# First outputs' chunks taken alternately, a seventh pair by seven products, and the last norm's shift and stores in quarters

## The chip, the cores and the metric

The kernel runs on one core of one Trainium2 chip. The metric is the device time of one execution in microseconds (us). Three runs of the kernel before took 716.66, 716.94 and 717.12 us. PE is TensorE (PEld its weight loads), DVE is VectorE, ACT is ScalarE, POOL is GpSimd, SP is the engine that issues most of the DMAs; each engine works through its own instructions in the order in which they were written.

## The reference

Two decoder layers over 256 tokens of width 1024, in float32:

```python
for l in range(DEPTH):                       # DEPTH = 2, x is (1, 256, 1024)
    mix = hybrid_mixer(x, w_in[l], w_branch_sb[l], w_branch_moba[l], w_out[l])
    x = layer_norm(ALPHA * x + mix, ln_mix_g[l], ln_mix_b[l])
    ffn = (silu(x @ w_gate[l]) * (x @ w_up[l])) @ w_down[l]      # inner width 2816
    x = layer_norm(ALPHA * x + ffn, ln_ffn_g[l], ln_ffn_b[l])
```

`hybrid_mixer` projects x to q, k, v of eight stick-breaking heads, q, k, v of eight softmax heads and two gates; each attention goes through its own output projection, the two are merged by the sigmoid gates and go through `w_out`. Nearly all of the time is in products of x, or of what was made of it, with weights.

## The kernel before

**Products.** Every float32 operand is split into a high part (cast to float32r, on ACT) and a low part (the rest, subtracted on DVE). A product is made of three matmuls: high with high, high with low, low with high (`mm3`). Tiles of 128 tokens are called t = 0 and t = 1.

**The weight stream.** The weights come in granules of 128 x 1024 numbers (512 KB), 122 of them a layer; `g` numbers them in the order of use, and `place` gives where a granule lies in memory. `WeightStream.load` issues the load of a granule into one of six raw tiles (`NRAW`) on SP's queue; `WeightStream.line` casts it on ACT into `whi` and subtracts on DVE into `wlo`, rings of ten granules each. A raw tile is free for the next load when its granule is split, a ring place when PE has used its granule. A few granules (`BY_DMA`) are split by DMA instead (`dma_line`): POOL issues a load into the high part, ACT makes its negative in the low part, and POOL issues a second load that adds the weights to it. `ASIDE` lists chunks of the last stage that are made in the same way, into other places than the ring; it is empty.

**The order of work** is fixed when the program is written: `Weave` keeps an estimate of each engine's time and emits side work (splits, loads, norms, attention) between the products when its due time has come. Nothing is reordered on the chip.

**Start.** x comes transposed in pieces (`xT_raw`; `x10` in `START` is token tile 1, piece 0). Four pieces go by ACT's queue, and then ACT loads its table for a first activation; the other two go by SP's. `START` is the order in which x's pieces and the halves of the first granules (`w10` is granule 1, half 0) are split. The first products are v of the stick-breaking heads (`pv`, granules 0 to 3) and then v of the other heads (`pu`, granules 4 to 7), each for both token tiles. `NWHOLE` = 1: granule 0 is multiplied unsplit, as float32, by `whole`.

**The last stage of a layer** multiplies the 22 chunks of h (128 of the 2816 inner columns each) with `w_down`. `DOWN[l]` is the order: an integer is a chunk taken singly (12 matmuls of 512 columns for each token tile's two halves together), a pair is taken by seven products instead of eight (21 matmuls instead of 24). For a pair the stream has the granules b and a, then two tiles of sums of halves, t and u, made on DVE by four additions of 512 columns (`raw<-raw`); of a only half is split. Sums of the two chunks of h are made on DVE earlier, as soon as both are there (`sums_line`). The last `HOLD[l]` chunks are kept for the end, where each token tile takes them by itself, so that the norm of tile 0 can start while PE works on tile 1. After the last pair, `combine_line` adds the seven products on DVE into x. The h tiles `h_t[i]` hold chunks 4i to 4i + 3, as a high and a low tile. The tiles of the norm's scale and shift, `ln` (`load_gb`), come from the same rotating pool of twelve as the twelve h tiles and are asked for right behind them; their loads are queued on SP when the sixth entry of `DOWN[l]` is reached (`n == 5`).

**The end.** `last_first` is the last norm of tile 0, `last_second` that of tile 1: x plus the products, statistics on DVE, a power on POOL, one scaling pass and one pass that multiplies and shifts (`x<-x,l1b_ve,ln`), each in two halves of 512 columns, and each half is stored by SP.

Of the kernel before, what the change touches and what calls it, by code (L numbers as in the profile page):

```python
# [7 lines left out]
F32 = mybir.dt.float32  # L8
F32R = mybir.dt.float32r
BF16 = mybir.dt.bfloat16  # L10
AF = mybir.ActivationFunctionType
OP = mybir.AluOpType
# [3 lines left out]
P = 128  # L16
# [14 lines left out]
GCOLS = 1024  # L31
NG_LAYER = 122
DOWN = ((0, (4, 5), (6, 7), 1, (8, 9), 2, (10, 11), 3, (12, 13), 14, 15, 16, 17, 18, 19, 20, 21),
        (0, (4, 5), (6, 7), 1, (8, 9), 2, (10, 11), 3, (12, 13), 16, (14, 15), 17, 18, 19, 20, 21))
STEPS = [[e for d in down for e in
          ([("n", d)] if isinstance(d, int) else [("b", d[1]), ("a", d[0]), ("t", d[0]), ("u", d[0])])]
         for down in DOWN]
BASE = [sum(NG_LAYER - NFC + len(x) for x in STEPS[:l]) for l in range(DEPTH + 1)]
EARLY = [*range(4), *range(16, 20), 8, 14, 9, 15, *range(4, 8), 20, 24, 21, 25, *range(10, 14), 22, 23,
         *range(26, 40)]  # L40
NACT = 12
# [67 lines left out]
class WeightStream:  # L109
# [2 lines left out]

    def __init__(self, nc, pool, w, total, weave, rings):
        self.nc, self.pool, self.w, self.total, self.weave = nc, pool, w, total, weave
        self.loaded, self.split = 0, NWHOLE
        self.done = -1
        self.free = {-1: 0.0}
        self.current = 0
        self.rings = rings
        self._lay()  # L120
        self.dma_t = 1.7
        self.raws, self.left = [], {0: 9.0}
        self.raw, self.parts, self.there, self.ready, self.dma = {}, {}, {}, {}, {}
# [50 lines left out]
    def by_dma(self, g):  # L174

        l, r = where(g)
        return r < NG_LAYER - NFC and r in BY_DMA[l] or self.aside(g)

    def aside(self, g):

# [3 lines left out]

    def put_aside(self, l, places):

        for g, parts in zip(filter(self.aside, range(BASE[l], BASE[l + 1])), places):
            self.parts[g] = parts
            self.dma[g] = self.weave.add(self.dma_line(g), self.weave.t)

    def dma_line(self, g):

        nc, weave = self.nc, self.weave
        hi, lo = self.parts[g]
        nc.gpsimd.dma_start(hi, self.w[place(g)], max_dma_last_dim=4096)
        yield weave.t + DMA_HI
        if self.aside(g):
            e = weave.pool(weave.t, nc.gpsimd.tensor_scalar, lo, hi.bitcast(F32), -1.0, None, op0=OP.mult) + 2.7
        else:
            e = weave.act(weave.t, GCOLS, nc.scalar.mul, lo, hi.bitcast(F32), -1.0)  # L200
        yield e
        nc.gpsimd.dma_start(lo, self.w[place(g)], accum_op=OP.add, max_dma_last_dim=4096)
        self.ready[g] = weave.t + DMA_LO

# [56 lines left out]
    def piece(self, g, i, e):  # L261

        if i == 0:
            self.parts[g] = tuple(ring[:, self.place[g]:self.place[g] + GCOLS] for ring in self.rings)
        (hi, lo), t, sl = self.parts[g], self.raw[g], self._pieces(g)[i]
        n = sl.stop - sl.start
        e = self.weave.act(e, n, self.nc.scalar.copy, hi[:, sl], t[:, sl])
        self.ready[g] = self.weave.dve(e, n, self.nc.vector.tensor_sub, lo[:, sl], t[:, sl], hi[:, sl].bitcast(F32))
        if sl.stop == GCOLS:
            self.raw.pop(g)  # L270
            self.left[g] = self.ready[g]
            self.split += 1
            self.load(g + 1 + NRAW)

# [6 lines left out]
    def take(self, g):  # L281
# [3 lines left out]
        while g in self.dma and g not in self.ready:  # L285
# [6 lines left out]
RING = 10 * GCOLS + LINES  # L292
NRAW = 6
NWHOLE = 1
START = (("x00", 4.4), ("x10", 5.4), ("x01", 6.4), ("w10", 6.4), ("w11", 7.4), ("x11", 7.4), ("w20", 8.2), ("x02", 9.0),
         ("w21", 9.7), ("x12", 10.3), ("w30", 11.0), ("w31", 11.7))
BY_DMA = ((18, 24, 28, 33, 38), (18, 24, 28, 33, 38))
ASIDE = ((), ())
X_AFTER = {(2, 0): (0, 2), (2, 1): (1, 2)}
NSPLIT = 10  # L300
HOLD = (8, 5)
FINE = 4
N_WARM = 10
LEAD = 2
# [14 lines left out]
def place(g):  # L319

    l, r = where(g)
    if r >= NG_LAYER - NFC:
        r = NG_LAYER - NFC + STEPS[l][r - (NG_LAYER - NFC)][1]
    return l * NG_LAYER + (EARLY[r] if r < len(EARLY) else r)


# [35 lines left out]
def hybrid_trunk_kernel(ctx: ExitStack, tc: tile.TileContext, w, xT_in, x_in, ln_in,  # L362
# [134 lines left out]

    kcs = [slice(0, 2), slice(2, 4), slice(4, 8)]
    ws.side = weave.add(ws.line(), last=True)
    for t, k in ((0, 0), (1, 0), (0, 1), (1, 1)):  # L500
        load_xT(t, kcs[k], nc.scalar)
    nc.scalar.activation(warm, zero, AF.Sigmoid)

    def between(g, i):
        if (g, i) in X_AFTER:
# [61 lines left out]

    def tok_major(o, g, t, first, last, k0):

        if g < NWHOLE:  # L570
            return whole(o, g, t, first)
        hi, lo = ws.take(g)
        hi = hi.rearrange("p (k c) -> p k c", k=2)
        lo = lo.rearrange("p (k c) -> p k c", k=2)
        for k in range(2):
            ts = slice(t * P, (t + 1) * P)
            mm3(o, xT_hi[:, k0 + k, ts], xT_lo[:, k0 + k, ts], hi[:, k, :], lo[:, k, :],
                first and k == 0, last and k == 1)

    def both_tokens(name, g0, put):  # L580

        acc = [banksB(f"{name}{t}")[:, 0, :] if g0 == 4 else bankM(f"{name}{t}", [P, WIDTH]) for t in range(2)]
        order = ((0, 0), (1, 0), (0, 1), (1, 1), (0, 2), (1, 2), (0, 3)) if g0 <= 4 else \
            ((0, 0), (0, 1), (0, 2), (1, 0), (1, 1), (0, 3), (1, 2))
        for t, k in order + ((1, 3),):
            tok_major(acc[t], g0 + k, t, k == 0, k == 3, 2 * k)
            if t == 1:
                ws.used(g0 + k)
            if k == 3:
                put(t, acc[t])  # L590

    def feat_major(o, g):

# [296 lines left out]
    def last_second(name, banks, gb, down):  # L890

        x = xs[1]
        st = small.tile([P, 3, 6], F32, tag="bn", name=f"{name}_bn1", bufs=1)
        mv = small.tile([P, 2], F32, tag="mv", name=f"{name}_mv1", bufs=1)
        ve = small.tile([P, 1], F32, tag="ve", name=f"{name}_ve1")
        cols = [halves[0], slice(512, 768), slice(768, 1024)]
        (_, first), (_, second) = banks
        rest = bankC(f"{name}_rest", [P, 512])[:, :256]
        down([(0, first)])
        residual(pe_done(), x, cols[0], first, scale=1.0)  # L900
        dve(0.0, 512, nc.vector.bn_stats, st[:, 0, :], x[:, cols[0]])
        down([(512, second)], NFC - HOLD[-1], NFC - FINE, last=False)
        down([(512, second[:, :256])], NFC - FINE)
        residual(pe_done(), x, cols[1], second[:, :256], scale=1.0)
        dve(0.0, 256, nc.vector.bn_stats, st[:, 1, :], x[:, cols[1]])
        residual(pe_done(), x, cols[2], second[:, 256:], scale=1.0)
        down([(768, rest)], NFC - FINE, first=True)
        dve(pe_done(), 256, nc.vector.tensor_add, x[:, cols[2]], x[:, cols[2]], rest)
        e = dve(0.0, 256, nc.vector.bn_stats, st[:, 2, :], x[:, cols[2]])
        e = dve(e, 16, nc.vector.bn_aggr, mv, st[:, :len(cols), :])  # L910
        e2 = dve(e, 16, nc.vector.tensor_scalar, ve, mv[:, 1:2], EPS, None, op0=OP.add)
        e2 = pool(e2, nc.gpsimd.tensor_tensor, ve, ve, mhalf, op=OP.pow)
        g, b = gb
        for c in halves:
            dve(e, 512, nc.vector.scalar_tensor_tensor, x[:, c], x[:, c], mv[:, 0:1], g[:, c], op0=OP.subtract, op1=OP.mult)
        for c in halves:
            dve(e2, 512, nc.vector.scalar_tensor_tensor, x[:, c], x[:, c], ve, b[:, c], op0=OP.mult, op1=OP.add)
            nc.sync.dma_start(out[P:, c], x[:, c])

    def v_parts(name):  # L920
        return [unit(f"{name}{t}", [P, 2 * NPAIR, 2, DH], F32R) for t in range(2)]
# [18 lines left out]
    for l in range(DEPTH):  # L940
# [10 lines left out]
            split_v(v_mb[t], ps)  # L951

        if l == 0:
            both_tokens(f"{L}pv", G, put_v)
            both_tokens(f"{L}pu", G + 4, put_u)
        else:
            for t in range(2):
                weave.finish(norms[:t + 1])
                pe_after(xT_ready[t])
                for j, put in enumerate((put_v, put_u)):  # L960
                    ps = bankM(f"{L}pvu{j}{t}", [P, WIDTH])
                    for i in range(4):
                        g = G + 4 * j + i
                        tok_major(ps, g, t, i == 0, i == 3, 2 * i)
                        if t == 1:
                            ws.used(g)
                    put(t, ps)
# [164 lines left out]

        pairs = [d for d in DOWN[l] if not isinstance(d, int)]
        pair_of = {c: i for i, p in enumerate(pairs) for c in p}
        raw_h, sums, h_there = {}, {}, {}

        def sums_line(i, e):

# [4 lines left out]
                                (3, b0, tmp[:, 1], OP.subtract)):  # L1143
                e = dve(e, P, nc.vector.tensor_tensor, tmp[:, j], x, y, op=op)
            if i < 2:
                both = wide_work(f"{L}hw{i}", F32R).rearrange("p a h c -> p (a h c)")[:, :GCOLS]
            elif i < 4:
                both = work.tile([P, 2, 2, S], F32R, tag=("sbq", "sbk")[i - 2],
                                 name=f"{L}hw{i}").rearrange("p a h c -> p (a h c)")
# [4 lines left out]
            elif i == 5:  # L1154
                places = [[x[:, 0::2, P:] for x in h_t[k]] for k in (1, 2)]
            else:
                places = [[x[:, 6:, :].rearrange("p k (j c) -> p (k j) c", c=P) for x in (xT_hi, xT_lo)]]
            n = 4 // len(places)
            sums[i] = [[hi_lo[m][:, j] for hi_lo in places for j in range(n)] for m in range(2)]
            yield e  # L1160
# [245 lines left out]
```

## Time and profile before

| what | value |
|---|---|
| median of three runs | 716.94 us |
| the profiled execution | 716.68 us, span 714.9 us |
| busy share of the span | PE 99%, PEld 92%, DVE 84%, ACT 61%, POOL 5% |
| granted TensorE clock | 0.997 |
| DMA | 141.58 MB, mean 198 GB/s over the span |

The span runs from the first to the last instruction. Lines of the order of time begin with the start and the length in us, then engine, line of the kernel, operation, the tiles written and read, and in brackets the idle time before with what ended it. Lines of waits name who waited for whom, the total, how often, and the longest. An engine's name with q is its sequencer, which issues DMAs.

### The profile page before, as it was taken

The numbers are of one execution on the slowest core, as the hardware profiler recorded it, in microseconds if no ns is written. First come the engines' busy times: TensorE is split into PE (matmuls) and PEld (weight loads), VectorE is DVE, ScalarE is ACT, GpSimd is POOL, SyncE is SP. The second block draws the span as 40 slices with busy tenths as digits, with TensorE's granted clock in tenths as the row PEclk, the third lists the DMA queues.
The fourth block names the chain that finished last, engine by engine and source line by source line (L and its number), as shares of the span: only waits on it lengthen the run. The fifth ranks groups of instructions, "written<-read, shape, count | busy, mean of one in ns | idle before, by whom it ended". The sixth has DMA issues, their size and how long they took to land. (4 is left out here: it accounts for less than half of the span.)

```text
span 714.9 us, 13082 instructions
## 1 busy us (share of the span) xinstructions
PE 706.7 (99%) x5135; PEld 657.7 (92%) x5135; DVE 599.5 (84%) x920; ACT 436.6 (61%) x677; POOL 35.0 (5%) x61
## 2 busy tenths in 40 slices
PE   9999999999999999999999999999999999999995
PEld 7999999998899999988889999999888999999885
DVE  5989989797888777799887899987879878778987
ACT  5868977664565554456456787876456555544551
POOL 0200100000000000000000010000010000000002
PEclk9999999999999999999999999999999999999998
DMA  8977755565585664449559566745646856524451
GB/s 319 396 230 254 198 153 173 167 217 186 171 301 197 194 194 145 122 142 329 198 183 315 155 186 170 213 142 177 237 147 216 273 189 198 191 96 137 147 206 59
DMA packets 40526, 141.58 MB, mean 198 GB/s; under 512 B 4625, under 2 KB 5393, under 8 KB 40465
## 3 DMA queue, kind: packets, MB, share of 16 engines
q1 hardware_dynamic: 37008, 129.74, 53.1%
q0 software_dynamic: 2880, 10.49, 6.9%
q8 instruction: 40, 0.66, 0.4%
q10 hardware_dynamic: 576, 0.52, 0.2%
q14 instruction: 22, 0.17, 0.1%
HBM read 139.69 MB, written 1.05 MB: 197 GB/s over the span
## 5 line engine op out<-in xcount | busy, mean ns | idle before, releaser
L65 DVE TENSOR_TENSOR wlo<-raw,whi 128x1024 fp32r<-128x1024 f32 (+1 forms) x274 | 302.2, 1125 | 27.2 <-ACT whi L60 23.8
L60 ACT CAST whi<-raw 128x1024 fp32r<-128x1024 f32 (+1 forms) x274 | 260.2, 973 | 75.1 <-DVE raw L65 29.5
L529 PE MATMUL l0pf<-xT_hi,whi 128*128 128x256 f32 x288 | 79.6, 276 | 0.0
L529 PE MATMUL l1pf<-xT_hi,whi 128*128 128x256 f32 x288 | 79.6, 276 | 0.0
L529 PE MATMUL l0pf<-xT_lo,whi 128*128 128x256 f32 x288 | 79.5, 276 | 0.0
L529 PE MATMUL l0pf<-xT_hi,wlo 128*128 128x256 f32 x288 | 79.5, 276 | 0.0
L529 PE MATMUL l1pf<-xT_hi,wlo 128*128 128x256 f32 x288 | 79.5, 276 | 0.0
L529 PE MATMUL l1pf<-xT_lo,whi 128*128 128x256 f32 x288 | 79.5, 276 | 0.0
L529 PEld LDWEIGHTS l0pf<-xT_lo,whi 128*128 128x128 f32 x288 | 54.1, 188 | 0.0
L529 PEld LDWEIGHTS l1pf<-xT_lo,whi 128*128 128x128 f32 x288 | 54.1, 188 | 0.0
L529 PEld LDWEIGHTS l1pf<-xT_hi,whi 128*128 128x128 f32 x288 | 54.1, 188 | 0.0
L529 PEld LDWEIGHTS l0pf<-xT_hi,whi 128*128 128x128 f32 x288 | 54.1, 188 | 0.0
L529 PEld LDWEIGHTS l0pf<-xT_hi,wlo 128*128 128x128 f32 x288 | 54.1, 188 | 0.0
L529 PEld LDWEIGHTS l1pf<-xT_hi,wlo 128*128 128x128 f32 x288 | 54.1, 188 | 0.0
L529 PE MATMUL l0pg<-xT_hi,whi 128*128 128x256 f32 x128 | 35.8, 280 | 0.0
L529 PE MATMUL l1pg<-xT_hi,whi 128*128 128x256 f32 x128 | 35.8, 280 | 0.0
L529 PE MATMUL l0pg<-xT_hi,wlo 128*128 128x256 f32 x128 | 35.5, 277 | 0.0
L529 PE MATMUL l1pg<-xT_hi,wlo 128*128 128x256 f32 x128 | 35.5, 277 | 0.0
L529 PE MATMUL l1pg<-xT_lo,whi 128*128 128x256 f32 x128 | 35.5, 277 | 0.0
L529 PE MATMUL l0pg<-xT_lo,whi 128*128 128x256 f32 x128 | 35.5, 277 | 0.0
L65 DVE TENSOR_TENSOR l1sf<-l1sf,l1pf 128x256 f32<-128x256 f32 x36 | 15.1, 421 | 15.5 <-ACT l1sf L60 14.9
L60 ACT ACTIVATE l0sf<-l0pf 128x256 f32<-128x256 f32 x18 | 6.9, 385 | 31.2 <-PE l0pf L529 31.2
(485 smaller groups left out, 1941.0 us busy)
## 6 DMA issues: line engine op xcount, KB each, us to landing
raw<-in_w_dram SPq DMA_DIRECT2D x230, 512.0 KB, 4.2
whi<-in_w_dram POOLq DMA_DIRECT2D x10, 512.0 KB, 5.1
wlo<-in_w_dram POOLq DMA_DIRECT2D x10, 512.0 KB, 6.3
ln<-in_ln_dram SPq DMA_DIRECT2D x8, 512.0 KB, 5.9
raw<-in_w_dram SPq DMA_DIRECT2D x8, 256.0 KB, 4.6
x<-in_x_dram SPq DMA_DIRECT2D x2, 512.0 KB, 4.7
xT_raw<-in_xT_dram ACTq DMA_DIRECT2D x4, 128.0 KB, 4.8
xT_raw<-in_xT_dram SPq DMA_DIRECT2D x2, 256.0 KB, 5.1
```

What stands on the lines that cost most here:

```text
L60: f(*args, **kw)
L65: f(*args, **kw)
L529: nc.tensor.matmul(o, a, b, start=start, stop=stop)
```

## The change

- **Start.** For layer 0 the granules of `pv` and `pu` are used alternately (`FIRST`), four accumulators at once: chunk i of both for both token tiles, before the next pieces of x. Granule 0 is multiplied unsplit for token tile 0 only; for tile 1 it is split like the others. ACT issues one x piece, then its table load, then three more pieces. The two x pieces on SP stand behind granule 3's halves instead of granule 2's.
- **Last stage of layer 1.** `(16, 17)` becomes a pair, so that there are seven; chunk 3 stands behind `(12, 13)`; chunks 2 and 3 are `ASIDE`, split by DMA into the x tiles, which are free by then, the second one's work due 3 us after the first's; four chunks instead of five are held for the end. The new pair's sums lie in the unused halves of the two wide tiles that hold the sums of the first two pairs.
- **End.** The last pass over tile 1 and its stores go in quarters of 256 columns, stores from ACT and SP in turn.

```diff
-        (0, (4, 5), (6, 7), 1, (8, 9), 2, (10, 11), 3, (12, 13), 16, (14, 15), 17, 18, 19, 20, 21))
+        (0, (4, 5), (6, 7), 1, (8, 9), 2, (10, 11), (12, 13), 3, (14, 15), (16, 17), 18, 19, 20, 21))
+FIRST = [0, 16, 1, 17, 2, 18, 3, 19]
...
-START = (("x00", 4.4), ("x10", 5.4), ("x01", 6.4), ("w10", 6.4), ("w11", 7.4), ("x11", 7.4), ("w20", 8.2), ("x02", 9.0),
-         ("w21", 9.7), ("x12", 10.3), ("w30", 11.0), ("w31", 11.7))
+START = (("x10", 4.8), ("w00", 4.9), ("x00", 4.9), ("w01", 5.4), ("w10", 6.1), ("w11", 6.7), ("w20", 7.4), ("x01", 7.4),
+         ("w21", 8.0), ("x11", 8.0), ("w30", 9.2), ("w31", 10.4), ("x02", 10.4), ("x12", 11.0))
-ASIDE = ((), ())
-X_AFTER = {(2, 0): (0, 2), (2, 1): (1, 2)}
+ASIDE = ((), (2, 3))
+X_AFTER = {(3, 0): (0, 2), (3, 1): (1, 2)}
-HOLD = (8, 5)
+HOLD = (8, 4)
...
-            self.dma[g] = self.weave.add(self.dma_line(g), self.weave.t)
+            self.dma[g] = self.weave.add(self.dma_line(g), self.weave.t + 3.0 * i)
...
-    for t, k in ((0, 0), (1, 0), (0, 1), (1, 1)):
+    load_xT(0, kcs[0], nc.scalar)
+    nc.scalar.activation(warm, zero, AF.Sigmoid)
+    for t, k in ((1, 0), (0, 1), (1, 1)):
         load_xT(t, kcs[k], nc.scalar)
-    nc.scalar.activation(warm, zero, AF.Sigmoid)
...
-        if g < NWHOLE:
+        if g < NWHOLE and t == 0:
             return whole(o, g, t, first)
...
+        acc = [[bankM(f"{names[0]}{t}", [P, WIDTH]) for t in range(2)],
+               [banksB(f"{names[1]}{t}")[:, 0, :] for t in range(2)]]
+        for i in range(4):
+            for n in range(2):
+                for t in range(2):
+                    tok_major(acc[n][t], g0 + 2 * i + n, t, i == 0, i == 3, 2 * i)
+                    if i == 3:
+                        puts[n](t, acc[n][t])
+                ws.used(g0 + 2 * i + n)
...
-        for c in halves:
-            dve(e2, 512, nc.vector.scalar_tensor_tensor, x[:, c], x[:, c], ve, b[:, c], op0=OP.mult, op1=OP.add)
-            nc.sync.dma_start(out[P:, c], x[:, c])
+        for i in range(4):
+            c = slice(i * D // 4, (i + 1) * D // 4)
+            dve(e2, D // 4, nc.vector.scalar_tensor_tensor, x[:, c], x[:, c], ve, b[:, c], op0=OP.mult, op1=OP.add)
+            (nc.sync if i % 2 else nc.scalar).dma_start(out[P:, c], x[:, c])
```

More of the change, by code (lines that the diff above doesn't have):

```diff
@@ L114, in __init__ @@
         self.nc, self.pool, self.w, self.total, self.weave = nc, pool, w, total, weave
-        self.loaded, self.split = 0, NWHOLE
+        self.loaded, self.split = 0, 0
         self.done = -1
@@ L176, in by_dma @@
         l, r = where(g)
-        return r < NG_LAYER - NFC and r in BY_DMA[l] or self.aside(g)
+        if r >= NG_LAYER - NFC:
+            return self.aside(g)
+        return r in BY_DMA[l]
     def aside(self, g):
@@ L185, in put_aside @@
     def put_aside(self, l, places):
-        for g, parts in zip(filter(self.aside, range(BASE[l], BASE[l + 1])), places):
+        for i, (g, parts) in enumerate(zip(filter(self.aside, range(BASE[l], BASE[l + 1])), places)):
             self.parts[g] = parts
-            self.dma[g] = self.weave.add(self.dma_line(g), self.weave.t)
+            self.dma[g] = self.weave.add(self.dma_line(g), self.weave.t + 3.0 * i)
     def dma_line(self, g):
@@ L196, in dma_line @@
         yield weave.t + DMA_HI
[L197 to L201, printed above, removed]
+        yield weave.act(weave.t, GCOLS, nc.scalar.mul, lo, hi.bitcast(F32), -1.0)
         nc.gpsimd.dma_start(lo, self.w[place(g)], accum_op=OP.add, max_dma_last_dim=4096)
@@ L269, in piece @@
         if sl.stop == GCOLS:
-            self.raw.pop(g)
-            self.left[g] = self.ready[g]
+            if g >= NWHOLE:
+                self.raw.pop(g)
+                self.left[g] = self.ready[g]
             self.split += 1
@@ L323, in place @@
         r = NG_LAYER - NFC + STEPS[l][r - (NG_LAYER - NFC)][1]
+    if l == 0 and r < len(FIRST):
+        return FIRST[r]
     return l * NG_LAYER + (EARLY[r] if r < len(EARLY) else r)
@@ L578, in tok_major, with both_tokens @@
                 first and k == 0, last and k == 1)
[L580 to L590, printed above, removed]
+    def both_tokens(names, g0, puts):
+        acc = [[bankM(f"{names[0]}{t}", [P, WIDTH]) for t in range(2)],
[7 more added lines that the diff above has]
+                ws.used(g0 + 2 * i + n)
     def feat_major(o, g):
@@ L953, in hybrid_trunk_kernel @@
         if l == 0:
-            both_tokens(f"{L}pv", G, put_v)
-            both_tokens(f"{L}pu", G + 4, put_u)
+            both_tokens((f"{L}pv", f"{L}pu"), G, (put_v, put_u))
         else:
@@ L1134, in hybrid_trunk_kernel @@
         pair_of = {c: i for i, p in enumerate(pairs) for c in p}
-        raw_h, sums, h_there = {}, {}, {}
+        raw_h, sums, h_there, wides = {}, {}, {}, []
         def sums_line(i, e):
@@ L1145, in sums_line @@
             if i < 2:
-                both = wide_work(f"{L}hw{i}", F32R).rearrange("p a h c -> p (a h c)")[:, :GCOLS]
+                both = wide_work(f"{L}hw{i}", F32R).rearrange("p a h c -> p (a h c)")
+                wides.append(both[:, GCOLS:])
             elif i < 4:
@@ L1156, in sums_line @@
             else:
-                places = [[x[:, 6:, :].rearrange("p k (j c) -> p (k j) c", c=P) for x in (xT_hi, xT_lo)]]
+                places = [[x.rearrange("p (j c) -> p j c", c=P) for x in wides]]
             n = 4 // len(places)
```

## The prediction

> **What bounds the kernel now.** I read the page's busy times first, then the waits of the weight loads (they and the matmuls share one sequencer), then the stage table near the end, then the order of time at both ends.
>
> ```profile
> PE 706.7 (99%) x5135; PEld 657.7 (92%) x5135; DVE 599.5 (84%) x920; ACT 436.6 (61%) x677; POOL 35.0 (5%) x61
> ...
> PEld l0pv L529 <- DVE xT_lo L65: 0.4, 1, 0.4
> ...
> 680.00:690.00 10.00, 10.00 (x46) 8.29 (x45) 8.76 (x11) 4.78 (x6) 0.00 (x0) 1.00 0.76 267
> 690.00:700.00 10.00, 10.00 (x46) 8.29 (x45) 8.87 (x10) 4.70 (x5) 0.00 (x0) 1.00 0.25 102
> ```
>
> PE is busy throughout, at the full granted clock, and its longest wait for data is 0.4 us, in the first product group. So removed products are worth their time unless something else is late. In layer 1's down stage (the windows; columns PE, PEld, DVE, ACT, POOL, clock, DMA share, GB/s) DVE is nearly as full as PE: that is the candidate for what is late next. The profiled execution took 716.68 us, of which 714.9 is the span; the median of the runs is 716.94, 0.26 more. My sum runs against 716.68.
>
> **Start.** Before: granule 0 unsplit for both token halves, then pv's and pu's products.
>
> ```profile
> 0.72 1.86 ACTq L490 DMA_DIRECT2D xT_raw<-in_xT_dram  x4
> 2.61 1.28 ACT L502 ACT_TABLE_LOAD   x1 [2.61 <-issue]
> 4.26 0.40 ACT L60 CAST xT_hi<-xT_raw 128x256 fp32r<-128x256 f32 x1
> 5.65 0.41 ACT L60 CAST xT_hi<-xT_raw 128x256 fp32r<-128x256 f32 x1 [0.99 <-DMA xT_raw<-in_xT_dram]
> 7.12 1.13 ACT L60 CAST whi<-raw 128x512 fp32r<-128x512 f32 x2
> 7.76 1.29 DVE L65 TENSOR_TENSOR wlo<-raw,whi 128x512 fp32r<-128x512 f32 x2
> ...
> 5.05 3.60 PE L564 MATMUL l0pv<-raw,xT_raw 128*128 128x512 f32 x8
> 8.08 0.80 PE L529 MATMUL l0pv<-whi,xT_hi 128*128 128x512 f32 x1
> 17.09 0.39 PE L529 MATMUL l0pu<-whi,xT_hi 128*128 128x512 f32 x1
> ...
> 15.51 4.97 DVE L65 TENSOR_TENSOR wlo<-raw,whi 128x1024 fp32r<-128x1024 f32 x4 [0.98 <-ACT whi L60]
> ...
> xT_raw<-in_xT_dram ACTq DMA_DIRECT2D x4, 128.0 KB, 4.8
> ```
>
> The eight unsplit passes step by 0.43 (5.05 to 8.48). A split product steps by 0.227 (the 55 steps from 681.24 to 693.70, shown below). The 36 of pv need 8.17, so pu could begin at 16.65; it begins at 17.09, 0.44 late, because x's slices are split only just in time. Taking v_sb's and v_mb's chunks alternately uses each x slice for twice as long, so that 0.44 should go. The second token half of granule 0 becomes six split products, 1.36 for 1.72: another 0.36 at most.
>
> Against it: that half now needs granule 0 split, and ACT takes x10 first. ACT's queue issued four loads in 1.86 (0.47 each) ahead of the table load; now the last three stand behind it and a short activation (table 1.28 from 2.61, the next cast at 4.26), so x10's issue moves from 1.2 to about 2.7. The casts at 4.26 and 5.65 show such loads landing some 1.4 apart, one after another, so x10 may still land at about 5.65; with 4.8 from issue it lands at 7.5. At 5.65: w00's cast starts some 0.35 later; with 0.52 a cast and 0.6 a subtraction, in the order x10, w00, x00, w01, w01's low part is ready at 8.2, and two products follow: 8.6 for 8.48 before. So 0.1 lost here and 0.44 won later. Ceiling: granule 4's low part is ready at 16.74 (15.51 and 1.23), and PE comes to it at 16.5 plus 0.23. I take -0.35; ends -0.6 and +1.5. The other start edits (waits on x02 and x12 two pieces later, granule 0 in the ring, its raw tile kept) cost nothing: x02 is needed near 16.5 instead of 11.2 (8.48 and 12 products).
>
> **Down stage of layer 1.** (16,17) becomes the seventh pair: 21 products for 24, so PE saves 3 x 0.227 = 0.68. Chunks 2 and 3 leave the raw-and-split stream; chunk 3 moves behind pair (12,13), and four chunks instead of five are held for the end.
>
> ```profile
> 630.43 0.88 DVE L65 TENSOR_TENSOR l1sf<-l1sf,l1pf 128x256 f32<-128x256 f32 x2 [2.64 <-ACT l1sf L60]
> 675.17 0.69 DVE L65 TENSOR_TENSOR raw<-raw 128x512 f32<-128x512 f32 x1
> 677.96 5.38 DVE L65 TENSOR_TENSOR wlo<-raw,whi 128x1024 fp32r<-128x1024 f32 x5
> 683.37 0.69 DVE L65 TENSOR_TENSOR raw<-raw 128x512 f32<-128x512 f32 x1
> 686.16 2.50 DVE L65 TENSOR_TENSOR wlo<-raw,whi 128x1024 fp32r<-128x1024 f32 x2
> ...
> L65 DVE TENSOR_TENSOR l1hs<-l1sf,l1hs x12: 283/288/293, 567.8 to 622.7; 128x128 f32<-128x128 f32 x12
> ...
> whi<-in_w_dram POOLq DMA_DIRECT2D x10, 512.0 KB, 5.1
> wlo<-in_w_dram POOLq DMA_DIRECT2D x10, 512.0 KB, 6.3
> ```
>
> - The pair's sums (four of 0.29, a 512 split of 0.7 on DVE and 0.6 on ACT) fall near 630, where DVE idles 2.64 at a time: nothing, while that cover lasts; without it 2.
> - Chunks 2 and 3: two DMAs each on POOL's queue and one ACT pass of 1.05; 5.1 + 1.05 + 6.3 = 12.5 from the end of the gate products (693.70 less 186 products of 0.227: 651.5) is 664, plus 3 for the second: 667. PE wants them at 671 and 683: hidden. ACT waiting for such a load, or the pass itself, may push a cast by 0.6; DVE's slack below covers it.
> - DVE: a pair with one single takes 8.2 (675.17 to 683.37); a single is 1.14, so a pair 7.06. Two such periods ahead of the group at 677.96 stand, at 661.56, the last two splits of pair (8,9), which end at 664.0; behind them follow now four pairs (28.2) and chunks 18 to 21 (4.6): 696.8. PE ends the last pair at 693.70 + 21 x 0.227 - 12 x 0.227 = 695.74. So no product waits for DVE's work itself, if the raw tiles are there.
>
> They are not, by these rows:
>
> ```profile
> 681.24 0.39 PE L529 MATMUL l1pe<-whi,l1h_lo 128*128 128x512 f32 x1
> 681.43 0.80 SPq L933 DMA_DIRECT2D ln<-in_ln_dram  x2
> 682.33 5.40 SPq L164 DMA_DIRECT2D raw<-in_w_dram  x5
> ...
> SPq L933 <- PE l1pe L529: 9.0, 1, 9.0
> ...
> 688.63 1.05 ACT L60 CAST whi<-raw 128x1024 fp32r<-128x1024 f32 x1 [1.23 <-DMA raw<-in_w_dram]
> 690.91 1.05 ACT L60 CAST whi<-raw 128x1024 fp32r<-128x1024 f32 x1 [1.23 <-DMA raw<-in_w_dram]
> 692.12 1.06 ACT L60 CAST whi<-raw 128x1024 fp32r<-128x1024 f32 x1 [0.16 <-DMA raw<-in_w_dram]
> 693.35 1.06 ACT L60 CAST whi<-raw 128x1024 fp32r<-128x1024 f32 x1 [0.18 <-DMA raw<-in_w_dram]
> 694.57 1.06 ACT L60 CAST whi<-raw 128x1024 fp32r<-128x1024 f32 x1 [0.15 <-DMA raw<-in_w_dram]
> ...
> 693.70 0.39 PE L529 MATMUL l1pd<-whi,l1h_hi 128*128 128x512 f32 x1
> 696.80 0.68 DVE L65 TENSOR_TENSOR l1pv<-l1pd,l1pv 128x512 f32<-128x512 f32 x1
> ```
>
> The last norm's two ln loads wait 9.0 on SP for PE, released as chunk 3's last product (681.24) ends: their tiles take over the first h pair, which holds chunks 0 to 3. The raw loads of chunks 17 to 21 stand behind them on SP; their casts each wait for the DMA (688.63 to 694.57), DVE's combination of the seven products waits behind the last split (696.80), and the final norm behind it. Moving chunk 3 back by one pair moves this release by 21 x 0.227 = 4.76, to 686.19, while the last pair's end moves by 2.04 only. Chunks 18 to 21 stand behind the ln loads too: their raw tiles come free when pairs (12,13) and (14,15) are split, after the ln loads are queued.
>
> So four casts follow the release as the first four did: +7.20, +9.48, +10.69, +11.92; the fourth's split on DVE ends 2.30 later (693.35 to 695.65, one 1.2 step ahead of 696.80's), and the combination follows at 686.19 + 14.22 = 700.41 for 696.80: +3.6. The gap of 2.28 between first and second cast is 1.06 above the others; whether it recurs the trace cannot say, so I take half of that off. Ends: +3.6, and no loss at all: ln's two and four raw tiles at the 1.22 of the later casts are there 7.3 after the release, at 693.5. I stay near the upper end, since the nearest rows are those very casts.
>
> The Trainium skill, DMA: Bandwidth & Descriptors, section "Anatomy of one DMA", says that DMA engines never wait on semaphores; the wait is on the issuing sequencer. By that rule the four raw loads cannot overtake the ln loads (700.4 for the combination); were each wait kept in its own transfer, they would go at the release of their tiles (696.8). The 9.0 on SP agrees with the rule.
>
> **End.** From the combination on DVE runs without a gap:
>
> ```profile
> 707.33 0.28 PE L529 MATMUL l1b_rest<-whi,l1h_lo 128*128 128x256 f32 x1
> 707.65 0.42 DVE L65 TENSOR_TENSOR x<-x,l1b_rest 128x256 f32<-128x256 f32 x1
> 710.37 1.40 DVE L65 SCALAR_TENSOR_TENSOR x<-x,l1b_ve,ln 128x512 f32<-128x512 f32 x2
> 711.14 0.99 SPq L918 DMA_DIRECT2D out_dram<-x  x2
> ...
> L65 DVE SCALAR_TENSOR_TENSOR x<-x,l1pe x3: 403/404/682, 705.0 to 707.1; 128x256 f32<-128x256 f32 x2, 128x512 f32<-128x512 f32 x1
> ...
> out_dram<-x SPq DMA_DIRECT2D x2, 256.0 KB, 2.0
> ```
>
> The last add starts 10.85 after the combination; PE's last product, started 0.32 before it, holds it by about 0.1. Afterwards PE would end at 707.61 - 0.68 = 706.93, DVE's chain at 700.4 + 10.7: DVE sets the end and the 0.68 is not seen. The shift in quarters: each 0.40 long and between 0.33 (half of 0.66) and 0.40 apart; with 0.37 the last ends at 710.37 + 3 x 0.37 + 0.42 = 711.9 for 711.77, +0.1. The last store is 128 KB instead of 256 and no longer stands behind a 256 KB one on its queue: its 2.0 falls to between 1.3 (a third off) and 2.0; I take 1.65. Together -0.25, ends -0.6 and +0.1. ACT, which issues two of the stores, is idle.
>
> The Trainium skill, DMA: Bandwidth & Descriptors, section "Issuing engines are not separate DMA queues", says a second issuing engine saves only issue time; issue (0.99 for two stores 0.66 apart: 0.33 each) is already covered here by the shifts, so by it only the smaller last store gains: -0.2 for -0.25, no other case.
>
> **Sum.** Start -0.35; combination +3.6 - 0.5 - 0.1 (PE's hold gone) = +3.0; stores -0.25: +2.4, so 716.68 + 2.4 = 719.1 us.
>
> **Rivals.**
> 1. The raw tiles are in time (they land earlier, or the loads are queued ahead of ln's). The point from which this decides: chunk 21's tile by 694.5, 8.3 after the release. Then DVE combines at 696.8 and adds at 707.5, or PE ends at 706.93: -0.1 to -0.68; with -0.35 and -0.25, 715.4 to 716.0. For it: 1.22 a tile once they flow. Against: the four casts that waited.
> 2. Half of that: tiles 1.5 to 2 us sooner than before, start and stores at their better ends: 717.1 to 718.
> 3. x10 lands 4.8 after its later issue, and ACT's whole queue waits behind it: start +1.5, 721.0. Against it: the 1.4 between landings.
> 4. The pair does nothing: product time is not the end's. That is within my forecast, where the 0.68 is lost.
>
> **Chances.** Forecast 0.60 (own range 718.0 to 720.2), first rival 0.15, second 0.17, third 0.08. The measurement tells 0.2%, 1.4 us, from no change: below 715.5 is faster, above 718.4 slower. Half the first rival is faster, with some good luck at both ends: 0.10; the second, the rest of the first and the low edge of the forecast are same: 0.28; slower 0.62. The range leaves out the lower half of rival one and the third: 715.6 to 720.4.
>
> **What would show it.** Right: ln's issue on SP right after chunk 3's last product and later, against the last pair's end, by 2.7; the last four casts waiting for DMA; the combination some 4 us behind PE's last pair; DVE without gaps to the last add and PE done well ahead of it. Wrong: raw loads of 18 to 21 issued ahead of ln's, or casts that wait for nothing; a PE wait in pv near 7 to 9 above 1 us; PE's last product again just ahead of the last add.

## The result and the profile after

The changed kernel takes 721.44 us (median of 5 runs, 720.69 to 722.08), the kernel before 717.09 in the same job (716.66 to 717.62): ratio 1.0060, 95% interval 1.0048 to 1.0071. It is slower by 4.3 us, where the prediction's sum was 2.4. The profiled execution took 720.69 us, the shortest of the five, with a span of 718.9, which is 4.0 longer than the span before.

The busy times of the page of after, then its waits of the weight loads and of SP's queue (waiter and what it waited for: total, times, longest):

```profile
PE 706.5 (98%) x5134; PEld 658.1 (92%) x5134; DVE 604.9 (84%) x933; ACT 439.2 (61%) x682; POOL 36.2 (5%) x65
...
PEld l0pq L532 <- DVE l0vsb L66: 1.5, 1, 1.5
...
SPq L937 <- PE l1pe L532: 14.5, 1, 14.5
```

PE does the same work as before (706.5 for 706.7 us busy), so the 4 us are not work of PE. Two waits stand out. One is new: the first product of q (`l0pq`) waits 1.5 us for the split of `pv`. The other is the ln issue on SP, 9.0 before and 14.5 now.

**The first place**, in the order of time at the end of the first products. After:

```profile
22.42 1.05 ACT L61 CAST whi<-raw 128x1024 fp32r<-128x1024 f32 x1 [0.94 <-DMA raw<-in_w_dram]
25.38 2.37 ACT L61 CAST whi<-raw 128x512 fp32r<-128x512 f32 x4 [0.21 <-DMA raw<-in_w_dram]
27.65 0.58 ACT L61 CAST l0vsb<-l0pv 128x512 fp32r<-128x512 f32 x1
28.75 0.68 DVE L66 TENSOR_TENSOR l0vsb<-l0pv,l0vsb 128x512 fp32r<-128x512 f32 x1
23.98 0.39 PE L532 MATMUL l0pv<-whi,xT_lo 128*128 128x512 f32 x1
28.06 0.39 PE L532 MATMUL l0pu<-whi,xT_lo 128*128 128x512 f32 x1
29.49 0.38 PE L532 MATMUL l0pq<-xT_hi,whi 128*128 128x256 f32 x1 [1.04 <-DVE l0vsb L66]
```

Before:

```profile
15.50 0.39 PE L529 MATMUL l0pv<-whi,xT_lo 128*128 128x512 f32 x1
20.40 1.46 DVE L65 TENSOR_TENSOR l0vsb<-l0pv,l0vsb 128x512 fp32r<-128x512 f32 x2
27.74 0.39 PE L529 MATMUL l0pu<-whi,xT_lo 128*128 128x512 f32 x1
27.97 0.28 PE L529 MATMUL l0pq<-xT_hi,whi 128*128 128x256 f32 x1
```

q's accumulator takes the `bankM` bank (a bank is a piece of the memory that PE sums into) in which `pv` of token tile 0 was summed. That sum is complete when the product at 23.98 ends, but its cast `l0vsb` stands on ACT behind casts of weights that themselves wait for DMA, and starts at 27.65; DVE's half of the split starts at 28.75 and ends at 29.43, and q starts at 29.49. Before, both tiles' splits were done at 21.86, 6.1 us ahead of q. Taken alternately, tile 0's last product of `pv` starts 8.5 us later (15.50 before); DVE's half of the split follows it about as late as before (4.8 us, 4.9 before), and so it now ends after PE is through with `pu`. The q product begins 1.52 later than before. Of this 1.2 is the wait, if q would else have followed the last product of `pu` (28.06) one step of 0.23 later; the other 0.3 is that this product itself came later than before (27.74).

**The second place**, the end of the down stage of layer 1 and what follows, in the order of time of after:

```profile
687.74 0.80 SPq L937 DMA_DIRECT2D ln<-in_ln_dram  x2
688.65 2.17 SPq L165 DMA_DIRECT2D raw<-in_w_dram  x4
694.86 1.05 ACT L61 CAST whi<-raw 128x1024 fp32r<-128x1024 f32 x1 [1.81 <-DMA raw<-in_w_dram]
696.10 1.06 ACT L61 CAST whi<-raw 128x1024 fp32r<-128x1024 f32 x1 [0.19 <-PE l1pt L532]
697.34 1.05 ACT L61 CAST whi<-raw 128x1024 fp32r<-128x1024 f32 x1 [0.18 <-DMA raw<-in_w_dram]
698.57 1.05 ACT L61 CAST whi<-raw 128x1024 fp32r<-128x1024 f32 x1 [0.18 <-DMA raw<-in_w_dram]
700.80 0.69 DVE L66 TENSOR_TENSOR l1pv<-l1pd,l1pv 128x512 f32<-128x512 f32 x1
708.21 0.28 PE L532 MATMUL l1b_rest<-whi,l1h_lo 128*128 128x256 f32 x1
711.63 0.42 DVE L66 TENSOR_TENSOR x<-x,l1b_rest 128x256 f32<-128x256 f32 x1
714.37 1.66 DVE L66 SCALAR_TENSOR_TENSOR x<-x,l1b_ve,ln 128x256 f32<-128x256 f32 x4
```

The ln loads are issued at 687.74: 681.43 before, plus 4.76 for the pair ahead of chunk 3, plus the start's 1.5. The four raw loads of chunks 18 to 21 follow them, and ACT casts one chunk after another from 694.86 on as the loads land (for the second cast the profile names a product of PE as what came last). The combination of the seven products starts at 700.80, 4.0 later than before (696.80); less the start's 1.5, the last stage itself adds 2.5. PE's last product ends 3.1 ahead of the last add (708.49 and 711.63); before, the two were 0.04 apart (707.61 and 707.65). The span's end is 4.53 behind the start of the last shift (714.37) as it was before (710.37 and 714.9).

So the profile gives: start +1.5, combination +2.5, end 0.

### The profile page after: what moved, and what is told of

It is laid out like the page before. It is cut to its first block, busy times and chain, and to the rows that moved or that the text cites. A ratio compares the mean times of both kernels' runs of the same rounds, so it can differ in the third digit from the quotient of the medians.

```text
span 718.9 us, 13099 instructions
## 1 busy us (share of the span) xinstructions
PE 706.5 (98%) x5134; PEld 658.1 (92%) x5134; DVE 604.9 (84%) x933; ACT 439.2 (61%) x682; POOL 36.2 (5%) x65
```

## The experiments

The two theories to be told apart at each place: the wait named above is the loss, or it only stands where something else (the pair's work on DVE, the order of the start, the quarters) would have cost the same.

**Chunk 3 behind (12,13), and nothing else, in the kernel before.** Does the position of the ln release alone make the kernel slow?

```diff
-(0, (4, 5), (6, 7), 1, (8, 9), 2, (10, 11), 3, (12, 13), 16, (14, 15), 17, 18, 19, 20, 21)
+(0, (4, 5), (6, 7), 1, (8, 9), 2, (10, 11), (12, 13), 3, 16, (14, 15), 17, 18, 19, 20, 21)
```

> The kernel before with one change: chunk 3 of layer 1 stands behind pair (12,13) instead of ahead of it; same products, same splits, five held chunks. Theory (ln's release by chunk 3): ln issued 4.8 us later, the combination of the seven products at about 701.5 instead of 696.8, time +4.6, 721.7. Rival (only the amount of work counts): 717.1.

Measured: 721.11 us, ratio 1.0062 (1.0050 to 1.0075). The waits on SP and the order of time of this kernel:

```profile
SPq L933 <- PE l1pe L529: 13.8, 1, 13.8
...
686.73 0.87 SPq L933 DMA_DIRECT2D ln<-in_ln_dram  x2
693.93 1.05 ACT L60 CAST whi<-raw 128x1024 fp32r<-128x1024 f32 x1 [5.98 <-DMA raw<-in_w_dram]
695.14 1.05 ACT L60 CAST whi<-raw 128x1024 fp32r<-128x1024 f32 x1 [0.16 <-DMA raw<-in_w_dram]
701.14 0.68 DVE L65 TENSOR_TENSOR l1pv<-l1pd,l1pv 128x512 f32<-128x512 f32 x1
```

One swapped entry in a list costs 4 us: the ln issue waits 13.8, the first cast behind it comes 7.20 after the release (7.20 before as well), and the combination 4.34 later than before, 0.55 of it because the stage begins later in this execution (first product at 652.06 for 651.51). PE, too, waits for the first chunk behind the release, 1.0 for its cast and 1.1 for its split. Here the five casts follow each other at 1.2, so the gap of 2.28 between the first two that the kernel before had is gone.

**The changed kernel with ln's loads queued later.** `late()` is called at the tenth entry of `DOWN[1]` instead of the sixth, so that the raw loads stand ahead of ln's on SP; nothing but SP's order differs.

```diff
-            if n == 5:
+            if n == (9 if l else 5):
                 late()
```

> The changed kernel with the last norm's two ln loads queued on SP four entries of the order of chunks later, behind the raw loads of chunks 18 to 21; PE, ACT and DVE keep their order. Theory (the ln loads' wait for chunk 3 holds the raw loads back): the casts of 18 to 21 no longer wait for DMA, DVE goes straight from the last pair's splits (694.3) through four splits of 1.15 to the combination near 698.8 instead of 700.8, and the time falls by about 2.0 us to 719.4. Rival (the seventh pair's own work on DVE makes the combination late): combination still at 700.8, time 721.4.

Measured: 718.78 us, ratio 1.0027 (1.0016 to 1.0037). The order of time:

```profile
678.46 8.68 SPq L165 DMA_DIRECT2D raw<-in_w_dram  x4
687.28 1.33 SPq L937 DMA_DIRECT2D ln<-in_ln_dram  x2
691.53 4.86 ACT L61 CAST whi<-raw 128x1024 fp32r<-128x1024 f32 x5 [0.40 <-DVE raw L66]
698.31 0.68 DVE L66 TENSOR_TENSOR l1pv<-l1pd,l1pv 128x512 f32<-128x512 f32 x1
707.75 0.28 PE L532 MATMUL l1b_rest<-whi,l1h_lo 128*128 128x256 f32 x1
709.14 0.42 DVE L66 TENSOR_TENSOR x<-x,l1b_rest 128x256 f32<-128x256 f32 x1
```

The last five casts run without waiting for a load, and the loss against the kernel before in the same job falls from 4.3 to 2.0 us. With the run before, this shows the queue order on SP as the cause of the last stage's part. Still DVE ends last: PE is done 1.1 ahead of the last add.

**The changed last stage alone.** Start and end are those of the kernel before; the seventh pair, chunk 3's place, the two chunks by DMA and the four held ones are those of after.

```diff
-        (0, (4, 5), (6, 7), 1, (8, 9), 2, (10, 11), 3, (12, 13), 16, (14, 15), 17, 18, 19, 20, 21))
+        (0, (4, 5), (6, 7), 1, (8, 9), 2, (10, 11), (12, 13), 3, (14, 15), (16, 17), 18, 19, 20, 21))
...
-ASIDE = ((), ())
+ASIDE = ((), (2, 3))
...
-HOLD = (8, 5)
+HOLD = (8, 4)
...
```

> Start and end as before, the changed last stage of layer 1 with ln's loads where the change has them (behind chunk 3). Theory: of the 4.3 us that the change costs, the last stage's part is the later release of ln alone, which moved the combination by 2.46 beyond the start: combination near 699.3 and last add near 710.1 in the profile, ratio about 1.0035 (719.5 us where the kernel before has 717.1). Rival: start and stage are not independent (the start's 1.5 delay is partly absorbed, or adds to the stage's), then 718 or less, or 720.5 and more.

Measured: 720.1 us, ratio 1.0036 (1.0022 to 1.0050). The order of time:

```profile
687.11 0.80 SPq L929 DMA_DIRECT2D ln<-in_ln_dram  x2
700.13 0.68 DVE L65 TENSOR_TENSOR l1pv<-l1pd,l1pv 128x512 f32<-128x512 f32 x1
```

The combination starts 3.33 later than before, but the stage itself begins 0.92 later in this execution (first product at 652.43 for 651.51), so 2.4 is the stage's own, as in after. Of the 0.92, 0.46 is there at q (28.43), and PE waits another 0.4 for a split in the last stage of layer 0. Such waits, 0.2 to 1.1 us long, are in eight of the twelve profiled executions, at a place that no edit touches; what makes them stays open.

**The changed start alone,** with the last stage and the end of the kernel before.

> The changed kernel's start with the last stage and the end of the kernel before. Theory (start costs 0.3 in the first products and 1.2 in the wait for pv's bank, and everything later moves with it): the first q product at 29.5 instead of 28.0, time +1.5, 718.6. Rival (later waits in the pipeline absorb a late start): 717.1 to 717.4.

Measured: 718.52 us, ratio 1.0028 (1.0018 to 1.0038); the eleven runs lie between 717.46 and 720.96. The same wait of q appears, longer in this execution. Waits and order of time:

```profile
PEld l0pq L532 <- DVE l0vsb L66: 2.4, 1, 2.4
...
30.18 0.39 PE L532 MATMUL l0pq<-xT_hi,whi 128*128 128x256 f32 x1 [1.99 <-DVE l0vsb L66]
```

The two halves together give 1.0028 and 1.0036, the whole 1.0060: the losses add up, within the intervals.

**The changed kernel with `pv` summed in the other banks.** Only where `pv` accumulates differs: `bankC`, which q does not take.

```diff
-        acc = [[bankM(f"{names[0]}{t}", [P, WIDTH]) for t in range(2)],
+        acc = [[bankC(f"{names[0]}{t}", [P, WIDTH]) for t in range(2)],
```

> The changed kernel with pv's two accumulators in the C banks instead of the M banks, each accumulator a tile of its own; pu stays in the B tiles, and the first q and k products get M banks that nothing holds. Theory (the only thing PE waits for at the first q product is pv's bank): the first q product starts right behind the last pu product, 1.2 to 2.4 earlier than in the changed kernel, time 720.0 +- 0.5. Rival (the late splits hold PE anyway, at the granules or at the next use of the C bank): a wait of the same length within the next 10 us, time 721.4.

Measured: 719.21 us, ratio 1.0030 (1.0018 to 1.0041). Its order of time and one of its waits:

```profile
27.87 0.28 PE L532 MATMUL l0pq<-xT_hi,whi 128*128 128x256 f32 x1
...
PEld l0pd L532 <- DVE wlo L66: 0.8, 1, 0.8
```

q starts at 27.87, without a wait, 1.6 us earlier than in after and 0.1 earlier than before. The bank was the wait. Half of the 1.6 is given back in layer 0's last stage in this execution (the 0.8), yet the loss against the kernel before in the same job falls from 4.3 to 2.0 us.

**A first attempt at the same, which missed.** All four accumulators in the two tiles of `banksB`, each of two banks: `pv` and `pu` of a token tile side by side.

```diff
-        acc = [[bankM(f"{names[0]}{t}", [P, WIDTH]) for t in range(2)],
-               [banksB(f"{names[1]}{t}")[:, 0, :] for t in range(2)]]
+        two = [banksB(f"{names[0]}{t}") for t in range(2)]
+        acc = [[two[t][:, n, :] for t in range(2)] for n in range(2)]
```

> The changed kernel with all four accumulators of the first outputs in the two-bank B tiles, so that the q products of the first pair get banks that nothing has used. Theory (PE's 1.2 us before the first q product is the bank that pv of token tile 0 still holds, whose split stands late in ACT's queue): the first q product starts at 28.3 instead of 29.5, and the time falls by 1.2 to 720.2. Rival (ACT and DVE are simply behind, and the wait moves to the next products or to the granules): PE waits as long a few us later, time 721.4.

Measured: 725.12 us, ratio 1.0113 (1.0098 to 1.0129). Waits, and the windows (columns PE, PEld, DVE, ACT, POOL, granted clock, DMA share, GB/s):

```profile
PEld l0pv L532 <- DVE l0vsb L66: 5.2, 1, 5.2
...
25.00:30.00 5.00, 0.30 (x2) 0.00 (x0) 5.00 (x8) 4.70 (x9) 0.00 (x0) 0.90 0.94 315
30.00:33.00 3.00, 2.89 (x7) 2.31 (x8) 1.86 (x4) 1.41 (x3) 0.00 (x0) 0.50 0.97 369
```

The edit made a wait of its own: with both sums of a token tile in one tile, the next write into that tile (a product of `pu`, which here bears the name `l0pv`) waits for the split of the first. It says nothing for or against the rival, but it does show how late the split is: PE was ready at 25.1 and got the bank at 30.

**The end in halves,** as before, in the changed kernel.

> The changed kernel with the last pass and its stores in two halves on SP, as before. By the traces the four quarters take 0.25 longer on DVE and the smaller last store wins 0.25 back. Theory: no difference, 721.4 +- 0.3. Rival (my estimate on record): the quarters win 0.25, 721.7; a gain of the store alone, 0.5 or more, would give 722.

Measured: 720.9 us, ratio 1.0054 (1.0042 to 1.0067), against 1.0060 (1.0048 to 1.0071) with quarters. Quarters and halves are not told apart; a gain of the quarters is not to be seen.

**What the pair is worth.** The changed last stage in the kernel before, with ln's loads queued later, so that neither of the two waits is there.

> The kernel before (its start, its end in halves) with the changed last stage of layer 1 and the ln loads queued four entries later. Theory (once the raw loads run free DVE's own work sets the end): combination near 697.2, last add near 708.0 for 707.65, PE's last product 0.7 earlier than before; time 717.3, 0.2 to 0.4 above the kernel before. Rival (the pair's 0.68 of PE time shows once nothing waits for ln): 716.3.

Measured: 717.35 us, ratio 1.0007 (0.9998 to 1.0016). The order of time:

```profile
661.14 1.06 ACT L60 ACTIVATE xT_lo<-xT_hi 128x1024 fp32r<-128x1024 f32 x1
663.17 2.96 DVE L65 TENSOR_TENSOR wlo<-raw,whi 128x1024 fp32r<-128x1024 f32 x3 [0.49 <-ACT whi L60]
697.13 0.68 DVE L65 TENSOR_TENSOR l1pv<-l1pd,l1pv 128x512 f32<-128x512 f32 x1
706.56 0.28 PE L525 MATMUL l1b_rest<-whi,l1h_lo 128*128 128x256 f32 x1
707.95 0.42 DVE L65 TENSOR_TENSOR x<-x,l1b_rest 128x256 f32<-128x256 f32 x1
```

PE finishes 0.77 earlier than before (706.56 for 707.33): the stage begins 0.09 earlier (651.42 for 651.51), and 0.68 is the three products saved. But the last add is at 707.95 for 707.65: DVE, for which the profile marks no wait between 663 and that add, sets the end, and the saved products are not seen.

**The same with less on DVE.** If DVE sets the end, taking work off it should bring the 0.77 in. x1 is scaled by POOL earlier, and two of the combination's additions for x1 go to POOL.

```diff
-            residual(e, x1, halves[0], r)
-            e = dve(e, 512, nc.vector.tensor_add, r, five, r)
-            residual(e, x1, halves[1], r, op=OP.subtract)
+            if l == 0:
...
+            else:
+                u = small_work(f"{L}pu2", [P, 512])
+                dve(e, 512, nc.vector.tensor_add, u, five, r)
+                pool(e, nc.gpsimd.tensor_scalar, x1, x1, ALPHA, None, op0=OP.mult)
+                pool(e, nc.gpsimd.tensor_tensor, x1[:, halves[0]], x1[:, halves[0]], r, op=OP.add)
+                pool(e, nc.gpsimd.tensor_tensor, x1[:, halves[1]], x1[:, halves[1]], u, op=OP.subtract)
```

> The same, with the two additions to x of token tile 1 in the combination taken from DVE (0.68 each) and given to POOL, which scales x of that tile beforehand. Theory (DVE's chain sets the end by about 1 us): DVE's chain becomes 1.4 shorter, PE's last product is again just ahead of the last add, time 716.3 to 716.5, 0.5 below the kernel before. Rival (the end hangs on something else, a DMA or PE): as the run without POOL, 717.3.

Measured: 717.59 us, ratio 1.0007 (0.9998 to 1.0015): a miss. The order of time:

```profile
664.29 3.59 POOL L70 TENSOR_SCALAR x<-x 128x1024 f32<-128x1024 f32 x1
664.01 3.80 DVE L65 TENSOR_TENSOR wlo<-raw,whi 128x1024 fp32r<-128x1024 f32 x3 [0.48 <-ACT whi L60]
700.83 1.29 POOL L70 TENSOR_TENSOR x<-x,l1pr 128x512 f32<-128x512 f32 x1 [32.95 <-DVE l1pr L65]
701.44 1.23 DVE L65 SCALAR_TENSOR_TENSOR x<-x,l1pv 128x512 f32<-128x512 f32 x1
703.79 0.68 DVE L65 SCALAR_TENSOR_TENSOR x<-x,l1pd 128x512 f32<-128x512 f32 x1
```

This execution enters the stage 0.84 later than the one above (652.26 for 651.42), so lengths are compared and not times. The stretch from the combination (698.80) to the last add (708.71) did get shorter, 9.91 instead of 10.82. But three splits beside POOL's scaling took 3.80 instead of 2.96, so DVE loses 0.84 ahead of it. The gain and the loss cancel; whether 0.77 could be had by relieving DVE in another way was not tried.

**Both repairs in the changed kernel:** ln's loads later and `pv` in `bankC`.

> The changed kernel with both repairs: ln's loads queued behind the raw loads, and the accumulators of the first product group in the other pair of banks, so that q's first product does not wait for their split. Theory: the two waits are all that the change costs, so the time is the kernel before's within 0.1%: 717.0 to 717.7, DVE setting the end with PE's last product 0.7 to 1.5 us ahead of the last add, and no wait at q. Rival: something else in the alternated start or the quarters costs 1 us or more beside the two waits: 718.2 or more.

Measured: 717.35 us, ratio 1.0006 (0.9997 to 1.0014). q starts at 27.87 and the last add at 708.15, 1.1 behind the end of PE's last product (706.77 and 0.28):

```profile
706.77 0.28 PE L532 MATMUL l1b_rest<-whi,l1h_lo 128*128 128x256 f32 x1
708.15 0.42 DVE L66 TENSOR_TENSOR x<-x,l1b_rest 128x256 f32<-128x256 f32 x1
```

Without the two waits the changed kernel can't be told from the kernel before. As far as 0.1% can be told they are the whole loss, and the rest of the change gains nothing that can be measured. No version that was run beats the kernel before.

## Why the prediction was right or wrong

The direction was right and the mechanism of the larger part was the forecast one; the size was not. Of the terms, against the profiled execution of before:

| term | predicted | after |
|---|---|---|
| start | -0.35 | +1.5 |
| combination | +3.0 | +2.5 |
| stores | -0.25 | 0 |
| sum | +2.4 | +4.0 |

- **Start: the step that failed.** The prediction counted when each granule, each x slice and each product would be ready, and named what hides the other start edits, but not the accumulators: it held nothing on when the bank of `pv` comes free for q. That wait cost 1.2 us of the +1.5 in the profiled execution, where the sum had a gain of 0.35; the weight loads wait 1.3 to 2.4 for it in the four profiled executions that have it. None of the prediction's signs of being wrong looks there. The rows that would have told it were in the trace of before: `l0vsb` split at 20.40, while tile 0's last product of `pv` starts at 15.50. With `pv` some 8 us later and the split late by as much as before, the split ends at q or behind it.
- **The range's upper end in the start (+1.5)** came from another cause, x10 landing late, and that did not happen. The prediction put x10's issue behind the table load, at about 2.7. In the trace of after, ACT's queue issues the three loads from 1.24 on, while the table load is running, and the first cast, of x10, starts at 5.44, 0.2 ahead of the 5.65 that the sum assumed. The third rival's 721.0 was thus near the measured time by luck, for a reason that the trace refutes.

```profile
1.17 1.28 ACT L503 ACT_TABLE_LOAD   x1 [1.17 <-PEq L1396]
1.24 1.35 ACTq L492 DMA_DIRECT2D xT_raw<-in_xT_dram  x3
5.44 0.40 ACT L61 CAST xT_hi<-xT_raw 128x256 fp32r<-128x256 f32 x1 [2.77 <-DMA xT_raw<-in_xT_dram]
```

- **The gain in the start** was -0.35 on paper and is not seen. The last product of `pu` starts at 27.64 to 28.06 in the six executions with the alternate order and separate tiles, and at 27.59 to 28.32 in the five with the start of before. With the bank's wait gone q starts 0.1 earlier than before (27.87 twice for 27.97).
- **Combination: right in its mechanism, 0.5 too large.** Beyond the start's 1.5 the release moved by 4.8, as computed; the last four casts came behind the loads that stand behind ln's; the first came 7.12 after the release (7.20 in the forecast). The term mis-sized is the gap of 2.28 between first and second cast, of which half was kept: it did not recur (the four follow at 1.24, the combination 13.06 after the release instead of 14.22), nor in chunk 3's run. In the run of the start alone, whose last stage is that of the kernel before, the first cast comes 8.55 after the release, no such gap follows, and the combination comes as late as before (15.51 after the release, 15.37 before). What holds the loads back in that stage stays open. The 0.1 for PE's hold on the last add was not there either: from the combination to that add it is 10.85 before and 10.83 after.
- **The 0.68 of PE not seen:** right. In the run of the changed stage with its loads in time, PE is 0.77 earlier and the time the same. So the first rival, which let PE or DVE end it at 715.4 to 716.0, was too hopeful even with the raw tiles in time. Its sum had DVE's last add at 707.5; it came at 707.95, mainly by the 0.49 that ACT's pass for the aside chunk makes DVE wait at 663, taken there as covered by slack. The gains that it took for the start and the stores were not found either.
- **Stores: -0.25 expected, nothing found.** The shift in quarters takes 1.66 for 1.40, 0.26 more where some 0.1 was computed, and the smaller last store gives only as much back (4.53 from shift to end in both).
- **What the Trainium skill says of DMA held:** the Trainium skill, DMA: Bandwidth & Descriptors, section "Anatomy of one DMA", puts the wait on the issuing sequencer. The 13.8 and 14.5 on SP agree with it, and so does the run in which only the order on SP was changed.

## What to carry to other kernels

A load that waits for a tile holds every load behind it on its queue, so moving a step that releases a tile is priced by what stands behind that wait: here one list entry cost 4 us, and calling one function four entries later gave 2.4 back in the changed kernel. When products are interleaved, all their accumulators end late together; look up when each bank's split was done before, by how much it lagged the products, and who takes the bank next. Saved products count only where PE, not DVE, does the last work.

## What the runs showed of the hardware that was not expected

- **DVE beside POOL.** An addition on DVE with both inputs in SBUF (`x<-x,l1pv`) took 1.23 instead of 0.69 while an addition ran on POOL, and ended 0.55 after it; one with an input in PSUM (`x<-x,l1pd`, 0.68) was not slowed beside a like addition on POOL from 703.35 on. The Trainium skill, SBUF — State Buffer, section "Who interferes with whom", says that a VectorE instruction with two SBUF inputs contends with a GpSimd instruction that reads SBUF, and calls the contention on the shared ports an exclusive lock. Both additions agree with it; the splits beside the scaling lost 0.84, far less than its 3.59, but spans on POOL are rough.
- **The clock after a wait.** In the kernel with `pv` and `pu` in shared tiles PE idled 5 us, and the granted clock in the next 3 us was 0.50. The Trainium skill, TensorE: Matmul & The Clock Gate, section "What's actually happening", has idle time of some 3.4 us lead to half rate; this agrees. The shorter wait of after left the clock at 1.00 (the columns as above):

```profile
28.00:30.00 2.00, 0.96 (x6) 0.54 (x6) 2.00 (x5) 2.00 (x5) 0.00 (x0) 1.00 0.96 307
```
